# Sums of weight blocks made in the first token group, in 128 columns, in buffers of the raw operands

## The chip, the core and the metric

The kernel runs on one core of one Trainium2 chip. TensorE (PE in the profile; PEld is its weight load) multiplies matrices, VectorE (DVE) and ScalarE (ACT) work on rows of elements, GpSimd (POOL) and SyncE (SP) mostly start transfers here. All engines take their instructions in a fixed order and wait for each other by semaphores. The metric is the device time of one execution in microseconds (us).

## The reference

One step of a layer whose heads are of two kinds. 1024 prompt frames and 8 x 16 frames of running streams (with 1024 cached frames each) go through the same weights:

```python
h = rms_norm(x, norm_pre)
p = einsum('btd,de->bte', h, w_in)         # D = 2048, 8 x 1024 columns
q_sb, k_sb, v_sb, gate_sb, q_r, k_r, v_r, gate_r = split(p)   # 8 heads of 128 each
o_sb = stick_breaking(q_sb, k_sb, v_sb)    # exp(log sigmoid(z) + sum of later log sigmoid(-z)) @ v
o_r, s = retention(rope(q_r), rope(k_r), v_r)   # chunks of 64, decayed state 128 x 128 per head
y = concat(head_norm(o_sb) * silu(gate_sb), head_norm(o_r) * silu(gate_r))
x = x + rms_norm(einsum('bte,ed->btd', y, w_out), norm_post)
```

Keys, values and states are returned too.

## The kernel before

**Two groups of tokens.** Group 0 is prompt tiles 0 to 3 and the sample tile (640 columns, multiplied in pieces of 256 and 384), group 1 is prompt tiles 4 to 7 (512 columns). Each group goes through the 8 heads. A head has the projections of its eight weight columns, a stick-breaking attention and a retention; in group 0 also the decode against the cached frames. After group 1 the output projection follows.

**Projections.** A chunk of weights `wr` (128x512) is loaded by SP (L369, five buffers) and split into a high part `wh` (ACT, L166) and a low part `wl` (DVE, L167). `products` (L380) then does four steps with three products each: wh with the high and the low part of the rows (`mh`, `ml`) and wl with the high part. The rows' projection does the same with `wrn`, `whn`, `wln` (L422, L436), in 10 steps for the 5 tiles of group 0.

**Jobs.** Everything else is written as generators. `Job(gen, wait)` puts one on a list, and `tick()`, called after each product, advances one of them when its countdown has run out. A generator yields the number of ticks until its next step, so the pace constants (`D_...`) spread its instructions between the products. `drain(job)` runs what is left of a job at once. `pin` ties an instruction to the matmul where it was written, without a semaphore. A scheduler then settles the order of each engine when the kernel is compiled; it is fixed at run time.

**What stands near the change.** The attention of a head makes scores, a scan of them (DVE, L660), a product (L661) and a transpose `kp<-be` (L721) that feeds the second product `pa` (PE, L761); `so<-pa` (L764) copies the result out. Retention runs over four tiles: scores `rs` (PE, L891), `sc` (DVE, L893), the output `pa` (PE, L909 and L914 with the state S), its copy `ro<-pa` (L912, L918), the state's product `pS` (PE, L924) and S (L927, L929). It needs the small decay table `dT` (SP, L886) and keys that come back from DRAM in another layout (`ro<-s_rk`, SP, L624).

**The sums.** The output projection is done with seven products of blocks instead of eight (L1175 to L1179). It needs sums and differences of blocks of w_out and of the rows y. `sum_weights` (L266) gives one item: two loads from w_out into a tile `br` of four blocks, four DVE operations between the blocks, one store to the scratch `s_b`. `sum_rows` (L277) is the same for rows, to `s_s`. `sums` (L285) runs a list of items, with the next item's loads issued before the present one's operations:

```python
nxt = fetch(items[i + 1][0]) if i + 1 < len(items) else None
for o, a, b, how in ops:
    pin(nc.vector.tensor_tensor(r[:, o], r[:, a], r[:, b], ALU.add if how == "a" else ALU.subtract))
    yield pace[0]
yield pace[1]
pin(nc.scalar.dma_start(dst, r))
```

The job is started in the attention of group 1's head 0, with 32 weight items of 256 columns and the 8 items of group 0's rows between them. `first_left` (L1043), which makes operands of the output projection, drains it.

The tag `mr` in the pool `wp` is four buffers of 128x512 for raw operands: `load_moving` (L244) uses them for the normalised rows of group 1 (`mr<-s_h`, L250), and the output projection uses them again.

Of the kernel before, what the change touches and what calls it, by code (L numbers as in the profile page):

```python
# [11 lines left out]
F32 = mybir.dt.float32  # L12
# [6 lines left out]
P = 128  # L19
D = 2048  # L20
KT = D // P
H = 8
# [36 lines left out]
D_FIN = 2  # L59
D_MR = 6  # L60
D_OP = 2
D_SUM2 = (4, 6, 36)
D_SUM3 = (3, 3, 6)
MR = 4
# [27 lines left out]
def tile_hybrid_step(  # L92
# [141 lines left out]
    def drain(job):  # L234
        while job is not None and not job.done:
            tick()
# [27 lines left out]
            yield D_MR  # L264

    def sum_weights(k, c):  # L266
        cs = slice(c * 256, (c + 1) * 256)

        def load(r):
            for kk in range(2):  # L270
                rows = w_out[0, (kk * HT + k) * P : (kk * HT + k + 1) * P, :]
                pin(nc.sync.dma_start(r[:, 2 * kk : 2 * kk + 2], rows.rearrange("p (a n) -> p a n", a=2)[:, :, cs]))

        ops = ((0, 1, 0, "s"), (1, 3, 1, "s"), (3, 3, 0, "s"), (2, 3, 2, "s"))
        return load, ops, s_b[c // 2][k][:, :, (c % 2) * 256 : (c % 2 + 1) * 256]

    def sum_rows(gi, h):  # L277
        def load(r):
# [3 lines left out]
        ops = ((3, 1, 3, "a"), (1, 0, 1, "s"), (0, 3, 0, "s"), (2, 2, 0, "s"))  # L282
        return load, ops, s_s[gi][h]

    def sums(pool, items, pace, bufs):  # L285

        def fetch(load):
            r = pool.tile([P, 4, 256], F32, name="br", tag="br", bufs=bufs)
            load(r)
            return r  # L290

        r = fetch(items[0][0])
        yield pace[2]
        for i, (_, ops, dst) in enumerate(items):
# [6 lines that stand above are left out]
            r = nxt  # L301
            yield pace[2]
# [147 lines left out]
    with ExitStack() as s1:  # L450
# [590 lines left out]
            return [[half[i][:, h // 2, h % 2 * 256 : h % 2 * 256 + 256] for h in range(HT)] for half in mov]  # L1041

        def first_left():  # L1043
            drain(summed[0])
            mine["s", 0] = [[half[h // WQ][:, h % WQ, NB_TOK:] for h in range(HT)] for half in mov]
            yield from left_sample(0, *mine["s", 0], wp, "mr", MR)
            mine[0, 5] = kept(0)
            yield from left(0, 5, *mine[0, 5], wp, "mr", MR)

        ret_job = sb_job = sub = loads = after = None  # L1050
        for gi, g in enumerate(GROUPS):
            tiles, n, nt = g["tiles"], g["n"], len(g["tiles"])
            if gi == 1:
                mov = after
            if gi:
                load_rope(gi)
            off = 0 if gi == 0 else 4
            phase[0] = gi
            for h in range(H):
                rows_in = {}  # L1060

                def ret_queries():
                    nonlocal ret_job, loads
                    if h == 0:
                        ret_values(g, mov, h, loads)
                        loads = None
                    acc = project(g, mov, col(4, h))
                    drain(ret_job)
                    rows_in["rq"] = rope(acc, "rq", *ropes)

                def ret_keys():
                    nonlocal ret_job
                    rk = rope(project(g, mov, col(5, h)), "rk", *ropes)
                    rows_in["rest"] = {}
                    ret_job = Job(
                        ret_branch(gi, g, h, rows_in["rq"], rk, pair["r"][:, :, h % 2, :], rows_in["rest"]),
                        D_NAT[phase[0]],
                    )

                def ret_start():  # L1080
                    nonlocal ret_job
                    rows_in["rest"] = first[-1]
                    ret_job = Job(ret_branch(gi, g, h, *first), D_NAT[phase[0]])

                def ret_gate():
                    rows_in["rest"]["rg"] = gate(project(g, mov, col(7, h)), "rg")

                def attention():
                    nonlocal sb_job, sub, ip
                    acc = project(g, mov, col(0, h))  # L1090
                    held = project(g, mov, col(1, h)) if h == H - 1 else None
                    drain(sb_job)
                    if gi == 1 and h == 0:
                        drain(sub)
                        late.close()
                        banks.append(s1.enter_context(tc.tile_pool(name="psx", bufs=1, space=PSUM)))
                        ip = s1.enter_context(tc.tile_pool(name="ip2", bufs=1))
                        items = [sum_weights(k, c) for k in range(HT) for c in range(4)]
                        items[8:8] = [sum_rows(0, h) for h in range(H)]
                        summed.append(Job(sums(ip, items, D_SUM2, 2), 8))  # L1100
                        Job(residuals(), 150)
                    q2 = [kq.tile([P, NB_TOK], F32R, name=f"q{c}", tag=f"q{c}") for c in "hl"]
                    evac_split(acc, *q2)
                    qs = None
                    if SAMPLE in tiles:
                        qs = kq.tile([P, P], F32, name="qs", tag="qs")
                        nc.scalar.activation(qs, acc[1][0][:, 2 * P : 3 * P], AF.Copy)
                    out = Out(4, "so")
                    rest = rows_in["sb"] = {}
                    if SAMPLE in tiles:  # L1110
                        drain(sub)
                        sub = Job(decode(h, qs, rest), D_DEC)
                    acc = held or project(g, mov, col(1, h))
                    kT = kq.tile([P, NMAX], F32, name="kT", tag="kT")
                    for a, (o, m) in acc:
                        nc.scalar.activation(kT[:, o : o + m], a[:, :m], AF.Copy)
                    pool, n = (ip, PT * P) if gi else (kq, NB_TOK)
                    k2 = [pool.tile([P, n], F32R, name=f"k{c}", tag=f"k{c}") for c in "hl"]
                    evac_split(acc, *k2, off * P)
                    if gi == 1:  # L1120
                        kp = wp.tile([P, NB_TOK], F32, name="kpast", tag="mr", bufs=MR)
                        nc.sync.dma_start(kp, s_k[h])
                        split(k2[0][:, :NB_TOK], k2[1][:, :NB_TOK], kp)
                    rest["kT"] = kT
                    sb_job = Job(sb_branch(gi, g, h, out, q2, k2, kT, rest), D_NAT[phase[0]])
                    if h % 2 == 0:
                        pair["s"] = ep.tile([P, 8, 2, P], F32, name="vn", tag="vn")
                        project_rows(g, mov, col(2, h), pair["s"], off)
                    vn = pair["s"][:, :, h % 2, :]
                    if gi == 1:  # L1130
                        nc.sync.dma_start(vn[:, :4, :], s_v[h])
                    rest["vn"] = vn

                def gates():
                    nonlocal after, loads
                    if h < H - 1:
                        rows_in["sb"]["sg"] = gate(project(g, mov, col(3, h)), "sg")
                        return

                    after = [[], []]  # L1140
                    loads = first_left() if gi else load_moving(after, 0, NB_TOK, from_h)
                    if gi == 0:
                        next(loads)
                    accs = project_pair(g, mov, (col(7, h), col(3, h)), loads)
                    rows_in["rest"]["rg"], rows_in["sb"]["sg"] = gate(accs[0], "rg"), gate(accs[1], "sg")


                if (gi, h) == (0, 0):
                    order = ret_start, attention, gates
                elif gi == 0 or h < H - 3:  # L1150
                    order = ret_queries, ret_keys, ret_gate, attention, gates
                elif h == H - 3:
                    order = ret_queries, ret_keys, attention, ret_gate, gates
                elif h == H - 2:
                    order = ret_queries, attention, ret_keys, ret_gate, gates
                else:
                    order = attention, ret_queries, ret_keys, ret_gate, gates
                for panel in order:
                    if panel is not ret_gate or h < H - 1:
                        panel()  # L1160
                if h % 2 == 1 and h < H - 1:
                    ret_values(g, mov, h + 1)
# [377 lines left out]
```

## Time and profile before

| | |
|---|---|
| three runs | 2297.01, 2302.54, 2304.21 us; median 2302.54 |
| profiled execution | 2303.65 us, span 2301.9 us, mean granted clock 0.996 |
| busy: PE, DVE, ACT, POOL | 98%, 54%, 40%, 16% of the span |
| DMA | 462.61 MB, mean 201 GB/s |
| DVE sums (`br`, 128x256) | 192 instructions of 0.419 us (median), from 1182.7 to 2056.6 us |
| loads of w_out for them, stores to `s_b` | 64 on SP from 1173.9 us, 32 on ACT to 1871.3 us |

All times in views are microseconds from the span's start, durations in "ns" are named so. A row of a timeline has start, duration, engine, line, operation and the tiles (out<-in); a bracket at its end is how long the engine was idle before it, and what ended that. "x2" is two instructions together. A row of waits has the waiting engine and line, what released it, the total, the number of times and the longest.

### The profile page before, as it was taken

What the parts mean: (1) busy time and instruction counts of PE and PEld (TensorE: products, weight loads), DVE (VectorE), ACT (ScalarE), POOL (GpSimd) and SP (SyncE); (2) the same over time, 40 slices, a digit from 0 to 9 for tenths busy, and PEclk for the clock granted to TensorE, in tenths of its full rate; (3) what the DMA queues carried; (4) which work ended last, traced back from release to release, by engine and by line L of the source; (5) the groups of instructions that cost most, each with busy time, mean ns of one, the idle gap of its engine ahead of it and who ended that gap; (6) DMA issues with size and microseconds to landing.
All of it is one profiled execution on the core that took longest, in us unless ns stands there. A gap on an engine that the chain in (4) does not pass through costs nothing.

```text
span 2301.9 us, 39303 instructions
## 1 busy us (share of the span) xinstructions
PE 2261.7 (98%) x14496; PEld 2045.1 (89%) x14496; DVE 1231.9 (54%) x2541; ACT 919.7 (40%) x1951; POOL 356.8 (16%) x601
## 2 busy tenths in 40 slices
PE   7999999999999999999999999999999999999998
PEld 7999999999999999999888889898889987888886
DVE  7335445344444435355556565656565566556567
ACT  6333333333333333334433343343443444535363
POOL 3002020111203012021202111120212212000020
PEclk9999999999999999999999999999999999999999
DMA  7547547566566757568769777778787767766586
GB/s 251 167 154 220 183 148 234 172 185 198 152 195 183 211 160 203 181 175 262 226 201 231 216 214 234 221 221 222 226 228 217 213 168 183 241 219 185 148 207 186
DMA packets 446497, 462.61 MB, mean 201 GB/s; under 512 B 181984, under 2 KB 309984, under 8 KB 444640
## 3 DMA queue, kind: packets, MB, share of 16 engines
q1 hardware_dynamic: 315952, 295.69, 44.7%
q0 software_dynamic: 28720, 78.41, 12.1%
q10 hardware_dynamic: 101632, 86.00, 11.9%
q8 instruction: 113, 1.85, 0.3%
q14 instruction: 80, 0.66, 0.1%
HBM read 355.12 MB, written 114.29 MB: 204 GB/s over the span
## 4 chain that ended last, share of the span: by engine, by line
PE 87%; DMA 6%; DVE 4%; issue 1%; ACT 1%; SPq 1%; POOL 0%; DVEq 0%; ACTq 0%; POOLq 0%
PE acc L380 45%; PE accn L436 17%; PE a L1178 5%; PE a L1179 5%; PE a L1175 5%; PE z L731 2%; PE pa L761 2%; PE zc L800 1%; DMA s_o<-so 1%; PE pd L864 1%; DMA ro<-s_rk 1%; PE pa L909 1%; DMA dT<-c_dt 1%; PE pS L924 1%; DMA s_rk<-rk 1%
## 5 line engine op out<-in xcount | busy, mean ns | idle before, releaser
L380 PE MATMUL acc<-mh,wh 128*128 128x256 f32 (+2 forms) x2304 | 663.6, 340 | 0.0
L380 PE MATMUL acc<-ml,wh 128*128 128x256 f32 (+2 forms) x2304 | 659.8, 339 | 0.0
L380 PE MATMUL acc<-mh,wl 128*128 128x256 f32 (+2 forms) x2304 | 657.0, 338 | 0.0
L167 DVE TENSOR_TENSOR wl<-wr,wh 128x512 fp32r<-128x512 f32 x504 | 346.4, 690 | 497.5 <-ACT wh L166 477.9
L166 ACT ACTIVATE wh<-wr 128x512 fp32r<-128x512 f32 x504 | 317.3, 631 | 654.2 <-PE acc L380 341.8
L380 PEld LDWEIGHTS acc<-ml,wh 128*128 128x128 f32 x2304 | 422.1, 188 | 31.2 <-issue 3.3
L380 PEld LDWEIGHTS acc<-mh,wl 128*128 128x128 f32 x2304 | 424.4, 188 | 27.7
L380 PEld LDWEIGHTS acc<-mh,wh 128*128 128x128 f32 x2304 | 420.4, 188 | 31.6 <-issue 3.3
L436 PE MATMUL accn<-whn,mh 128*128 128x256 f32 x1152 | 329.8, 286 | 0.0
L436 PE MATMUL accn<-wln,mh 128*128 128x256 f32 x1152 | 326.0, 283 | 0.0
L436 PE MATMUL accn<-whn,ml 128*128 128x256 f32 x1152 | 325.6, 283 | 0.0
L436 PEld LDWEIGHTS accn<-whn,mh 128*128 128x128 f32 x1152 | 220.7, 192 | 3.0 <-issue 0.8
L436 PEld LDWEIGHTS accn<-wln,mh 128*128 128x128 f32 x1152 | 220.8, 192 | 0.8
L436 PEld LDWEIGHTS accn<-whn,ml 128*128 128x128 f32 x1152 | 220.5, 192 | 0.0
L167 DVE TENSOR_TENSOR wln<-wrn,whn 128x512 fp32r<-128x512 f32 x128 | 87.8, 688 | 152.4 <-ACT whn L166 151.1
L166 ACT ACTIVATE whn<-wrn 128x512 fp32r<-128x512 f32 x128 | 80.7, 633 | 192.9 <-PE accn L436 86.9
L624 POOL DMA_DIRECT2D be<-s_be x128 | 94.1, 742 | 148.2 <-DMA s_be<-be 125.3
L660 DVE TENSOR_TENSOR_SCAN kp<-kp 128x1152 f32<-128x1152 f32 (+4 forms) x40 | 82.8, 2069 | 51.5 <-POOL kp L649 35.0
L649 POOL TENSOR_SCALAR_AFFINE_SELECT kb<-kb 128x128 f32<-128x128 f32 x64 | 30.5, 484 | 451.2 <-ACT kb L643 448.9
L787 POOL DMA_DIRECT2D kcT<-cache_k x64 | 34.7, 545 | 422.7 <-PE pd L864 268.8
L1178 PE MATMUL a<-wl,mh 128*128 128x512 f32 x240 | 93.5, 390 | 0.0
L1179 PE MATMUL a<-wh,ml 128*128 128x512 f32 x240 | 93.6, 390 | 0.0
(257 smaller groups left out, 3001.9 us busy)
## 6 DMA issues: line engine op xcount, KB each, us to landing
wr<-w_cols SPq DMA_DIRECT2D x384, 256.0 KB, 4.3
wrn<-w_rows SPq DMA_DIRECT2D x128, 256.0 KB, 3.4
kcT<-cache_k POOLq DMA_DIRECT2D x64, 512.0 KB, 8.0
vc<-cache_v SPq DMA_DIRECT2D x64, 512.0 KB, 5.5
wr<-s_b SPq DMA_DIRECT2D x80, 256.0 KB, 4.4
br<-w_out SPq DMA_DIRECT2D x64, 256.0 KB, 5.2
s_b<-br ACTq DMA_DIRECT2D x32, 512.0 KB, 4.9
wr<-w_out SPq DMA_DIRECT2D x48, 256.0 KB, 3.9
```

The costliest lines, as they stand in the source:

```text
L166: nc.scalar.activation(hi, src, AF.Copy),
L167: nc.vector.tensor_tensor(lo, src, hi.bitcast(F32), ALU.subtract),
L380: last = nc.tensor.matmul(a[:, :m], lhs[:, j, :], rhs[w][:, j, o : o + m], start=(w == 0 and j == 0 and n == 0), stop=(w == KT // WQ - 1 a ...
L436: anchor[0] = nc.tensor.matmul(a, lhs[q][:, jj, ts], rhs[:, j, :], start=(w == 0 and j == 0 and n == 0 and t % 2 == 0), stop=(w == KT // 2 ...
L624: q.dma_start(raw[32 * i : 32 * i + 32, :].rearrange("p (k a) -> p k a", a=32), s[:, :, 32 * i : 32 * i + 32].rearrange("k (j b) a -> b (k ...
L660: nc.vector.tensor_tensor_scan(rev, rev, rev, 1.0, ALU.mult, ALU.bypass)
L731: nc.tensor.matmul(z[:, :c], q2[a][:, i * P : (i + 1) * P], k2[b][:, s : s + c], start=(m == 0), stop=(m == 2),)
L761: nc.tensor.matmul(po[:, :P], at[:, j, :], vn[:, j, :], start=(j == 0), stop=(j == t))
L787: ready.append((kc, nc.gpsimd.dma_start(kc, cache_k[h, m // 4, m % 4])))
L1175: ins = nc.tensor.matmul(a, hi[k][:, ts], wh, start=first, stop=False)
L1178: nc.tensor.matmul(a, hi[k][:, ts], wl, start=False, stop=False)
L1179: anchor[0] = nc.tensor.matmul(a, lo[k][:, ts], wh, start=False, stop=last)
```

## The change

The weight sums become 64 items of 128 columns instead of 32 of 256. Their tile is 128 x 4 x 128, the size of an `mr` buffer, and they take the four `mr` buffers in turn (tag "mr" in pool `wp`). They are started in the attention of group 0's head 1, with a pace of their own. In group 1's head 0 this job is drained, and there a second job is started for the 8 items of rows alone, as before in 128x256 with two buffers in the pool `ip2`. `first_left` drains that second job.

```diff
+D_SUM0 = (4, 4, 14)
 D_SUM2 = (4, 6, 36)
...
     def sum_weights(k, c):
-        cs = slice(c * 256, (c + 1) * 256)
+        cs = slice(c * P, (c + 1) * P)
...
-        return load, ops, s_b[c // 2][k][:, :, (c % 2) * 256 : (c % 2 + 1) * 256]
+        return load, ops, s_b[c // 4][k][:, :, (c % 4) * P : (c % 4 + 1) * P]
...
-    def sums(pool, items, pace, bufs):
+    def sums(pool, items, pace, bufs, tag="br", n=256):
...
-            r = pool.tile([P, 4, 256], F32, name="br", tag="br", bufs=bufs)
+            r = pool.tile([P, 4, n], F32, name="br", tag=tag, bufs=bufs)
...
         def first_left():
-            drain(summed[0])
+            drain(summed[1])
...
-                        items = [sum_weights(k, c) for k in range(HT) for c in range(4)]
-                        items[8:8] = [sum_rows(0, h) for h in range(H)]
-                        summed.append(Job(sums(ip, items, D_SUM2, 2), 8))
+                        drain(summed[0])
+                        summed.append(Job(sums(ip, [sum_rows(0, h) for h in range(H)], D_SUM2, 2), 8))
                         Job(residuals(), 150)
+                    if (gi, h) == (0, 1):
+                        items = [sum_weights(k, c) for k in range(HT) for c in range(8)]
+                        summed.append(Job(sums(wp, items, D_SUM0, MR, "mr", P), 8))
```

Lines of the changed kernel stand one higher than those of before in the code that the rows below name (L381 is L380).

**Group 0, head 2, TensorE.** Retention of this head, before; `acc` rows are products of weight chunks:

```order
L380 MATMUL acc_4505<-ml_174,wh 128x256
L380 MATMUL acc_4506<-ml_174,wh 128x384
L380 MATMUL acc_4505<-mh_173,wl 128x256
L380 MATMUL acc_4506<-mh_173,wl 128x384
L891 MATMUL rs<-rq,rk 128x128
L909 MATMUL pa<-rv,sc 128x128
L914 MATMUL pa<-S,rq 128x128
L380 MATMUL acc_4505<-mh_173,wh 128x256
```

After, at the same retention's first steps:

```order
L910 MATMUL pa<-rv,sc 128x128
L925 MATMUL pS<-rv,rkn 128x128
L892 MATMUL rs<-rq,rk 128x128
L910 MATMUL pa<-rv,sc 128x128
L915 MATMUL pa<-S,rq 128x128
L381 MATMUL acc_4382<-mh_179,wh 128x256
L381 MATMUL acc_4383<-mh_179,wh 128x384
L381 MATMUL acc_4382<-ml_180,wh 128x256
L381 MATMUL acc_4383<-ml_180,wh 128x384
L925 MATMUL pS<-rv,rkn 128x128
L381 MATMUL acc_4382<-mh_179,wl 128x256
```

Before, a step of retention (three or fewer short matmuls) stands between products of chunks that are under way; after, five short matmuls of two steps stand directly ahead of a chunk's first products, and pS of the second step inside it. Such places are found in heads 2 to 7 of group 0; those of group 1 are as before.

**The same place on VectorE**, before (`sg` is work of the finishing of another head):

```order
L893 TENSOR_TENSOR sc<-rs,dT 128x128 x2
L695 SCALAR_TENSOR_TENSOR sg<-kT,gains,sg 128x512
L912 COPY ro<-pa 128x128
L927 COPY S<-pS 128x128
L167 TENSOR_TENSOR wl<-wr,wh 128x512 x2
```

After:

```order
L894 TENSOR_TENSOR sc<-rs,dT 128x128 x2
L913 COPY ro<-pa 128x128
L928 COPY S<-pS 128x128
L894 TENSOR_TENSOR sc<-rs,dT 128x128
L168 TENSOR_TENSOR wl<-wr,wh 128x512 x2
L919 SCALAR_TENSOR_TENSOR ro<-pa,dec,ro 128x128
L168 TENSOR_TENSOR wl<-wr,wh 128x512
```

The score products and copies of two steps now stand together ahead of the `wl` conversions, and one more score product is among them.

**The loads ahead of that place, on SP's queue**, before (`ro`, `so` and `dT` belong to retention and to the finishing of heads; `vc` is the cached values):

```order
L827 DMA vc<-cache_v 128x1024 x2
L369 DMA wr<-w_cols 128x512 x2
L827 DMA vc<-cache_v 128x1024 x2
L369 DMA wr<-w_cols 128x512 x2
L624 DMA ro<-s_rk_2_4153 32x20x32 x4
L624 DMA so<-s_o_1_4_0_4233 32x16x32 x4
L886 DMA dT<-c_dt 128x256
L369 DMA wr<-w_cols 128x512 x2
L422 DMA wrn<-w_rows 128x512 x5
```

After:

```order
L273 DMA br<-w_out 128x2x128 x2
L828 DMA vc<-cache_v 128x1024 x2
L370 DMA wr<-w_cols 128x512
L273 DMA br<-w_out 128x2x128 x2
L370 DMA wr<-w_cols 128x512
L625 DMA ro<-s_rk_2_4218 32x20x32 x4
L625 DMA so<-s_o_1_4_0_4314 32x16x32 x4
L273 DMA br<-w_out 128x2x128 x2
L887 DMA dT<-c_dt 128x256
L370 DMA wr<-w_cols 128x512 x5
L423 DMA wrn<-w_rows 128x512 x4
```

The loads of w_out stand between the others, and ahead of `ro` there are two single `wr` loads where two pairs stood; behind `dT` there are five where two stood.

**Group 1, head 2, VectorE**, ahead of the transpose `kp<-be` 128x896, before:

```order
L474 TENSOR_TENSOR rq<-rq,sw 128x512
L297 TENSOR_TENSOR br<-br 128x256
L764 COPY so<-pa 128x128
L660 SCALAR_TENSOR_TENSOR kp<-kp 128x1024
L297 TENSOR_TENSOR br<-br 128x256
L661 TENSOR_TENSOR be<-be,kp 128x1024
L297 TENSOR_TENSOR br<-br 128x256
L721 STREAM_TRANSPOSE kp<-be 128x896
```

After:

```order
L475 TENSOR_TENSOR rq<-rq,sw 128x512
L765 COPY so<-pa 128x128
L168 TENSOR_TENSOR wl<-wr,wh 128x512
L661 SCALAR_TENSOR_TENSOR kp<-kp 128x1024
L639 MEMSET kp 128x1
L662 TENSOR_TENSOR be<-be,kp 128x1024
L722 STREAM_TRANSPOSE kp<-be 128x896
```

The three sums are gone, and a `wl` conversion stands ahead of the scan.

## The prediction

> **What bounds the kernel now.** I read the page's busy times first, then the busy table of two stretches, then TensorE's waits in them. The columns of the table are: the stretch, its length, busy time (and instructions) of PE, PEld, DVE, ACT and POOL, the granted clock, the busy share of the DMA engines, GB/s.
>
> ```profile
> PE 2261.7 (98%) x14496; PEld 2045.1 (89%) x14496; DVE 1231.9 (54%) x2541; ACT 919.7 (40%) x1951; POOL 356.8 (16%) x601
> 310.00:1060.00 750.00, 749.32 (x5727) 713.92 (x5726) 338.76 (x740) 263.03 (x569) 126.22 (x232) 1.00 0.63 187
> 1174.00:1870.00 696.00, 687.72 (x3947) 604.79 (x3946) 419.64 (x792) 270.66 (x562) 124.80 (x196) 1.00 0.79 220
> PE pa L761 <- DVE kp L721: 6.2, 5, 2.3
> PE pa L909 <- DVE so L764: 1.6, 2, 1.3
> PE pa L914 <- DVE S L929: 0.4, 1, 0.4
> ```
>
> TensorE is the bound: 98% busy, at full clock in both stretches. The first stretch is heads 1 to 7 of the first group. TensorE is idle there for 750.00 - 749.32 = 0.7 us. The second stretch is the second group while it makes the weight sums, and TensorE is idle for 696.00 - 687.72 = 8.3 us. The three last rows name nearly all of that: 6.2 + 1.6 + 0.4 = 8.2 us, always behind DVE, which is busy for 420 of 696 us there and for only 339 of 750 us in the first stretch. The change takes no matmul away. So it can gain at most about these 8.2 us, and it can lose wherever it makes TensorE wait in a stretch that has no waits yet.
>
> **What leaves the second group.** The work that moves:
>
> ```profile
> L297 DVE TENSOR_TENSOR br<-br x192: 379/419/514, 1182.7 to 2056.6; 128x256 f32<-128x256 f32 x192
> L272 SPq DMA_DIRECT2D br<-w_out x64: 540/602/1649, 1173.9 to 1843.1; - x64
> L300 ACTq DMA_DIRECT2D s_b<-br x32: 520/582/1346, 1190.2 to 1871.3; - x32
> ```
>
> Of the 192 DVE instructions 4 x 32 = 128 are weight sums (the other 64 sum rows, and stay): 128 x 0.419 = 53.6 us of DVE. That is almost all of the second stretch's surplus. What it is worth is read where TensorE waits, at the transpose that feeds the second product of the attention:
>
> ```profile
> 1265.79 1.25 DVE L721 STREAM_TRANSPOSE kp<-be 128x1024 f32<-128x1024 f32 x1 [3.58 <-DMA be<-s_be]
> ...
> 1345.51 0.42 DVE L297 TENSOR_TENSOR br<-br 128x256 f32<-128x256 f32 x1
> 1345.85 0.28 DVE L764 COPY so<-pa 128x128 f32<-128x128 f32 x1
> 1346.05 2.28 DVE L660 TENSOR_TENSOR_SCAN kp<-kp 128x1024 f32<-128x1024 f32 x1
> 1348.25 0.40 DVE L297 TENSOR_TENSOR br<-br 128x256 f32<-128x256 f32 x1
> 1348.56 1.22 DVE L661 TENSOR_TENSOR be<-be,kp 128x1024 f32<-128x1024 f32 x1
> 1349.70 0.42 DVE L297 TENSOR_TENSOR br<-br 128x256 f32<-128x256 f32 x1
> 1350.04 1.10 DVE L721 STREAM_TRANSPOSE kp<-be 128x896 f32<-128x896 f32 x1
> ...
> 1454.39 0.69 DVE L167 TENSOR_TENSOR wl<-wr,wh 128x512 fp32r<-128x512 f32 x1 [1.24 <-DMA br<-w_out]
> 1351.19 1.05 PE L761 MATMUL pa<-vn,kp 128*128 128x128 f32 x7 [0.74 <-DVE kp L721]
> ...
> 1459.68 1.50 PE L761 MATMUL pa<-vn,kp 128*128 128x128 f32 x11 [1.06 <-DVE kp L721]
> ```
>
> Three sums stand in the chain from copy to transpose of head 2 (0.42 + 0.40 + 0.42 = 1.24 us). In the new order a 0.69 us wl conversion moves up into that gap, so the chain shortens by about 0.55 and not by 1.24. At head 3 DVE even stands still for 1.24 us in a sum that waits for its load. That and the sums around it are more than the 1.06 us for which TensorE waits. Of the 6.2 us the longest wait, 2.3, has no sum in its chain: its transpose stood idle for a load, be<-s_be (first row). Of the other 3.9 I take 3.2. The copy so<-pa stands right behind a sum as well, so I take 1.2 of its 1.6. **Gain: 4.4 us**, with bounds 0 (each chain keeps another late link) and 8.2 (all waits go, the 2.3 by a quicker load once 33.5 MB less share the DMA engines).
>
> **What comes into the first group.** 64 items of 128 columns: 256 DVE instructions, 128 loads on SP, 64 stores on ACT, the same bytes. One item takes 4 x 4 + 4 + 14 = 34 ticks. The list starts at head 1's attention, near 300 us. The rows for its cost:
>
> ```profile
> L893 DVE TENSOR_TENSOR sc<-rs,dT 128x128 f32<-128x128 f32 x28 | 7.3, 278 | 12.0 <-PE rs L891 9.9 <-DMA dT<-c_dt 2.1
> L167 DVE TENSOR_TENSOR wl<-wr,wh 128x512 fp32r<-128x512 f32 x140 | 96.4, 689 | 181.0 <-ACT wh L166 180.1 <-PE rs L891 0.9
> L167 DVE TENSOR_TENSOR wln<-wrn,whn 128x512 fp32r<-128x512 f32 x42 | 29.1, 692 | 75.0 <-ACT whn L166 74.8
> L166 ACT ACTIVATE wh<-wr 128x512 fp32r<-128x512 f32 x140 | 88.3, 631 | 233.9 <-PE acc L380 166.2 <-PE accn L436 35.3 <-DMA wr<-w_cols 11.6
> wr<-w_cols SPq DMA_DIRECT2D x384, 256.0 KB, 4.3
> out<-vn ACTq DMA_DIRECT2D x16, 256.0 KB, 3.2
> out<-kT ACTq DMA_DIRECT2D x16, 256.0 KB, 4.1
> ```
>
> A wl chunk is 12 ticks and a wln chunk 10, so the 140 and the 42 of these rows are 1680 + 420 = 2100 ticks in 750 us, 0.357 each. An item is then 12.1 us, and the list 775: over near 1075, ahead of 1173.9, where it only began before.
>
> - DVE: a 128x128 operation takes 0.278, so 256 x 0.278 = 71 us, 18 more than leave. With 339 + 71 = 410 of 750 us DVE is as full as it is in the second group now. Cost taken: nothing by itself, since the wl conversions wait 180 us for ACT and not for DVE.
> - ACT: 64 issues at 0.52 to 0.58 (the store's shortest and median above) are 33 to 37 us beside 263 of 750. Nothing, for the wh conversions wait for TensorE to free buffers (166.2).
> - SP: 128 issues at 0.54 to 0.60, or 69 to 77 us, in a queue that also carries every weight load. They can delay those loads; the bunches below price that.
> - DMA: 33.5 MB in 775 us is +43 GB/s on 187, and the busy share goes from 0.63 to about 0.63 x 230/187 = 0.78, the second group's level now. Rows of 512 bytes in the sums are no surcharge: the vn store writes such rows and takes 3.2 us, the kT store of equal size with 2 KB rows 4.1.
>
> Order shows one thing that the counts don't. From head 2 on, retention stands in a bunch right ahead of a weight chunk, with that chunk's wl behind the retention's own work on DVE. There are six such places (heads 2 to 7). Before, this work was spread between products:
>
> ```profile
> 375.41 7.35 SPq L624 DMA_DIRECT2D ro<-s_rk  x4
> 382.86 2.04 SPq L624 DMA_DIRECT2D so<-s_o  x4
> 384.94 0.49 SPq L886 DMA_DIRECT2D dT<-c_dt  x1
> 395.18 0.39 PE L909 MATMUL pa<-rv,sc 128*128 128x128 f32 x2
> 395.40 0.39 PE L924 MATMUL pS<-rv,rkn 128*128 128x128 f32 x2
> 395.60 0.29 DVE L912 COPY ro<-pa 128x128 f32<-128x128 f32 x1 [1.55 <-PE pa L909]
> 395.82 0.29 DVE L927 COPY S<-pS 128x128 f32<-128x128 f32 x1
> 1167.78 0.49 PE L909 MATMUL pa<-rv,sc 128*128 128x128 f32 x2 [0.31 <-DVE ro L918]
> ```
>
> The price of one bunch. After pS, DVE has the two copies (0.29 each), a score product (0.28) and the wl conversion (0.69): 1.55 us. TensorE meanwhile has three short matmuls (0.22 from one start to the next, 395.18 to 395.40) and two ticks of 0.357: 1.37 us. So it waits 0.2, and the one bunch of this kind in the trace waits 0.31 (last row). 0.3 is the lower end. If the chunk's wh is not ready either, 0.63 is added: 0.9. If a second and a third conversion stand behind it as well, 2 x 0.69 more: 2.3. I take 0.9: wr loads now stand in the queue behind ro, so and dT, which hold SP for 375.41 to 385.4, about 10 us, so wh loses its head start. **Loss: 6 x 0.9 = 5.4 us**, with bounds 1.8 and 13.8.
>
> At the boundary of the groups the first four mr<-s_h loads now wait for the sums' buffers; the last w_out loads stand ahead of them and the wait for the list costs no tick. I take nothing (0 to 1.5).
>
> **Sum.** -4.4 + 5.4 = +1.0. The profiled run took 2303.65 us (span 2301.9), so it would become 2304.7. That run lies 1.1 us above the median of 2302.54. I name 2304, between the sums from either. About 0.3%, or 6.9 us, is what a measurement of this kernel can tell from no change.
>
> **The rivals.**
> - A, faster: the first group hides everything, bunches too, and the second loses all its waits. 2303.65 - 8.2 = 2295.4. For it: 0.7 us of idle time in 750. Against: the bunches are in the order, and nothing stands behind the wl there.
> - B, slower: weights become late at the bunches. The next chunk's wr stands behind the held queue, and its head start must cover landing 4.3 plus wh 0.63 = 4.9 us. Five buffers of 12 ticks are 5 x 4.3 = 21 us of head start at most. The new order has three such loads fewer ahead of the held entries: 21 - 13 = 8 us is left. It decides when the entries hold SP for 3 to 4 us longer than their 10 now. The price of one wait of that length is in the clock as well:
>
> ```profile
> 1932.01 0.49 PE L909 MATMUL pa<-rv,sc 128*128 128x128 f32 x2 [2.05 <-DVE so L764]
> 1932.00:1937.00 5.00, 5.00 (x20) 4.23 (x21) 1.67 (x5) 2.59 (x10) 2.73 (x4) 0.66 0.79 172
> ```
>
>   After a wait of 2.05 us the clock (the column after POOL's) was 0.66 for the next 5 us: 0.34 x 5 = 1.7 us more. Six waits of 2.1 cost 6 x 3.8 = 22.8, less the gain 4.4: +18, or 2322.
>   The Trainium skill (TensorE: Matmul & The Clock Gate, Part 1) says that the clock is lowered only after a whole idle window of some 3.4 us. By that the six waits would cost 6 x 2.1 = 12.6 and the case +8. The clock fell after 2.05 us here, so the measurement decides and the 1.7 stay in.
> - C, slower: the first group takes over the second's way of waiting, since DVE (410 of 750) and DMA (0.78) come to the same level. 8.2 us in 696 become 9.1 in 775; with the bunches 5.4 and the gain 4.4 that is +10, or 2314. Against: its attention chains are shorter (four tiles of rows with at most 512 keys), so fewer transposes come late.
> - That the change does nothing isn't open: order moves all 64 items ahead of the boundary.
>
> **How the numbers follow.** The forecast, within 0.3%, gets 0.42: its own range is 2297 to 2309. A gets 0.18, B 0.22, C 0.18. B is likelier than C because its rows stand in the order. Low: 2295, which takes A's point in. High: 2322, B's point; half of B and a little of A lie outside, under 2 in 10. Faster 0.18, same 0.42, slower 0.22 + 0.18 = 0.40.
>
> **What would show it.** Right: in the second group the waits of pa for kp fall to the 2.3 of head 1 and something under 1; in the first group six waits of 0.3 to 2.3 us before L381 or pa, for wl or S; a DMA share near 0.78. Wrong: waits of L381 for wh behind wr<-w_cols of over 2 us with a granted clock of 0.66 after them (B); waits for kp and so spread over heads 1 to 7 (C); no waits in the first group at all (A).

## The result

The changed kernel took 2338.82 us in the median of four runs (2333.81 to 2344.24), the kernel before 2301.01 us. The ratio is 1.0157, with a 95% interval from 1.0137 to 1.0178: slower by 38 us by the medians and 36 by the ratio, outside the range that was given and beyond rival B.

The span and the busy line of the changed kernel's page (its profiled execution took 2344.24 us):

```profile
span 2342.5 us, 39517 instructions
PE 2276.4 (97%) x14496; PEld 2056.6 (88%) x14496; DVE 1241.6 (53%) x2669; ACT 918.6 (39%) x1951; POOL 359.8 (15%) x601
```

Two stretches of its busy table, columns as in the prediction. The first lies in the first group, the second in the second group, without weight sums:

```profile
310.00:1085.00 775.00, 751.40 (x5634) 713.20 (x5634) 382.69 (x960) 256.75 (x557) 124.39 (x228) 0.98 0.74 215
1200.00:1900.00 700.00, 692.28 (x4015) 606.74 (x4014) 377.20 (x680) 273.23 (x574) 125.39 (x195) 1.00 0.63 174
```

The span grew by 2342.5 - 2301.9 = 40.6 us. TensorE's idle time went from 2301.9 - 2261.7 = 40.2 us to 2342.5 - 2276.4 = 66.1 us, which is 25.9 of it. The other 14.7 us are busy time of the same 14496 matmuls, at a lower clock (0.98 in the first stretch). The loss lies in the first group: 775.00 - 751.40 = 23.6 us idle there. The second group is idle for 7.7 us, where it was 8.3.

TensorE's waits in the whole changed kernel, without those of the start; columns as in the prediction:

```profile
PE pa L910 <- DVE sc L894: 23.1, 6, 5.7
...
PE pa L762 <- DVE kp L722: 7.2, 5, 3.3
PE acc L381 <- ACT wh L167: 3.8, 3, 2.4
```

Six waits of retention's output matmul for its scores `sc`, one in each of heads 2 to 7, make 23.1 us. They are at the places that order had shown, but for another reason than the one named. Here is head 2 in the changed kernel's timeline:

```profile
375.19 6.97 SPq L625 DMA_DIRECT2D ro<-s_rk  x4
382.33 3.35 SPq L625 DMA_DIRECT2D so<-s_o  x4
385.73 3.97 SPq L273 DMA_DIRECT2D br<-w_out  x2
389.74 0.60 SPq L887 DMA_DIRECT2D dT<-c_dt  x1
...
395.43 0.49 DVE L894 TENSOR_TENSOR sc<-rs,dT 128x128 f32<-128x128 f32 x2 [3.80 <-DMA dT<-c_dt]
395.78 0.80 PE L910 MATMUL pa<-rv,sc 128*128 128x128 f32 x2 [4.73 <-DVE sc L894]
396.04 0.63 ACT L167 ACTIVATE wh<-wr 128x512 fp32r<-128x512 f32 x1 [6.27 <-DMA wr<-w_cols]
```

VectorE and ScalarE have nothing to do: VectorE waits 3.80 us for the table dT, ScalarE 6.27 us for a weight chunk. dT is issued at 389.74, where the kernel before issued it at 384.94, and it lands 5.6 us later where it took 3.5. The transfers are late, not an engine's work.

A part of each wait comes from TensorE's own order. Counted in the two traces, retention's first `pa` stands 13 matmuls of `acc` and `accn` earlier in the changed kernel, in each of heads 2 to 7. From 375 to 395 the kernel before has 119 of these matmuls in 20 us, so 13 are about 2.2 us (an estimate). With `pa` at its old place and dT as late as here, about 11 of the 23.1 us would be left. No run changes this place alone.

A long wait can be paid twice. The busy table of the changed kernel, 5 us from the end of a wait on, after the waits of 4.73, 0.95, 2.37 and 4.13 us:

```profile
395.80:400.80 5.00, 5.00 (x22) 5.00 (x23) 4.04 (x11) 3.27 (x9) 0.00 (x0) 0.53 0.73 229
...
810.90:815.90 5.00, 2.52 (x16) 2.01 (x16) 1.45 (x6) 1.29 (x5) 0.00 (x0) 1.00 0.60 196
816.00:821.00 5.00, 5.00 (x24) 5.00 (x25) 3.58 (x9) 2.10 (x5) 0.00 (x0) 0.66 0.84 289
951.90:956.90 5.00, 4.96 (x21) 4.96 (x22) 4.04 (x11) 3.27 (x9) 0.00 (x0) 0.51 0.71 229
```

The clock is whole after 0.95 us, 0.66 after 2.37, and about a half after more than 4. There are six such places (five at waits for sc, one at the wait for wh). Over the 5 us behind each they had a clock of 0.53, 0.67, 0.50, 0.66, 0.51 and 0.50, which loses 13.2 us, most of the 14.7.

### The profile page after: what moved, and what is told of

Its sections match the earlier page's. It is cut to its first block, busy times and chain, and to the rows that moved or that the text cites. A ratio compares the mean times of both kernels' runs of the same rounds, so it can differ in the third digit from the quotient of the medians.

```text
span 2342.5 us, 39517 instructions
## 1 busy us (share of the span) xinstructions
PE 2276.4 (97%) x14496; PEld 2056.6 (88%) x14496; DVE 1241.6 (53%) x2669; ACT 918.6 (39%) x1951; POOL 359.8 (15%) x601
## 4 chain that ended last, share of the span: by engine, by line
PE 83%; DMA 8%; DVE 4%; issue 2%; ACT 2%; SPq 1%; ACTq 0%; POOL 0%; DVEq 0%; POOLq 0%
PE acc L381 42%; PE accn L437 17%; PE a L1181 5%; PE a L1182 5%; PE a L1178 5%; PE pa L762 2%; DMA wr<-w_cols 2%; PE z L732 2%; DMA dT<-c_dt 2%; PE zc L801 1%; DMA s_o<-so 1%; PE pa L910 1%; DMA s_b<-br 1%; DVE wl L168 1%; PE pS L925 1%
## 5 line engine op out<-in xcount | busy, mean ns | idle before, releaser
L381 PE MATMUL acc<-mh,wh 128*128 128x256 f32 (+2 forms) x2304 | 663.8, 341 | 4.9 <-ACT wh L167 3.8
L381 PE MATMUL acc<-ml,wh 128*128 128x256 f32 (+2 forms) x2304 | 661.0, 340 | 0.0
L381 PE MATMUL acc<-mh,wl 128*128 128x256 f32 (+2 forms) x2304 | 660.3, 340 | 0.0
L381 PEld LDWEIGHTS acc<-mh,wh 128*128 128x128 f32 x2304 | 423.3, 189 | 37.5 <-ACT wh L167 4.5
L381 PEld LDWEIGHTS acc<-ml,wh 128*128 128x128 f32 x2304 | 424.5, 189 | 30.3 <-issue 2.1
L381 PEld LDWEIGHTS acc<-mh,wl 128*128 128x128 f32 x2304 | 424.4, 189 | 29.1 <-issue 1.2
L298 DVE TENSOR_TENSOR br<-br 128x128 f32<-128x128 f32 (+1 forms) x320 | 99.9, 313 | 7.0 <-DMA br<-s_y 4.0
```

What stands on the lines that cost most here:

```text
L381: last = nc.tensor.matmul(a[:, :m], lhs[:, j, :], rhs[w][:, j, o : o + m], start=(w == 0 and j == 0 and n == 0), stop=(w == KT // WQ - 1 a ...
```

## The experiments

All ratios are to the kernel before, with 95% intervals. The first theory was that SP's queue is the cause: 128 loads of w_out stand in it ahead of dT and the weights.

**Loads on another queue.**

```diff
-                pin(nc.sync.dma_start(r[:, 2 * kk : 2 * kk + 2], rows...
+                pin(nc.gpsimd.dma_start(r[:, 2 * kk : 2 * kk + 2], rows...
```

> The changed kernel with the 128 loads of w_out for the sums issued by GpSimd and not by SyncE; operations, stores and bytes are the same. Theory Q (the six waits of TensorE for sc come from SP's queue: the loads of w_out stand ahead of dT, ro and wr there and hold them up): no wait of pa for sc over 1 us is left in the first group, and the time is 2297 to 2306. Rival D (the 43 GB/s more on the DMA engines make dT and wr land late, whoever issues them): the waits stay, 2325 to 2345. Rival V (256 operations more on VectorE in the first group): the waits stay, 2325 to 2345.

2336.3 us, ratio 1.015 (1.0132 to 1.0168). The theory of SP's queue fell. The waits in the first group:

```profile
PE pa L910 <- DVE sc L894: 26.2, 6, 5.5
```

In this kernel's order the bunches of the first group are gone as well: no place there has more than three matmuls of retention in a row, and the first `pa` stands within 2 matmuls of its old place. Two weight loads stand right ahead of ro, as before the change. SP's rows in head 2:

```profile
371.25 0.86 SPq L370 DMA_DIRECT2D wr<-w_cols  x2
372.16 12.35 SPq L625 DMA_DIRECT2D ro<-s_rk  x4
384.62 4.43 SPq L625 DMA_DIRECT2D so<-s_o  x4
389.09 0.56 SPq L887 DMA_DIRECT2D dT<-c_dt  x1
```

The landing times of dT in heads 2 to 7 (least, median, greatest, in us):

```profile
DMA to landing us min/median/max: 7.7/8.3/11.7
```

In head 2 the four issues of ro took 12.35 us, where they took 7.35 in the kernel before. The median landing of dT was 8.3 us, where it was 5.3. So late transfers make waits of this size without the bunches and without loads of w_out in SP's queue. What the bunches cost in the changed kernel is not measured by that.

**Loads alone.**

```diff
-                pin(nc.vector.tensor_tensor(r[:, o], ...
+                n == P or pin(nc.vector.tensor_tensor(r[:, o], ...
...
-            pin(nc.scalar.dma_start(dst, r))
+            n == P or pin(nc.scalar.dma_start(dst, r))
```

> The changed kernel with the loads of w_out alone: the 256 operations and the 64 stores of the weight sums are left out, and the output projection reads single blocks of w_out where it read sums (as many bytes). Q: the loads alone make the waits for sc, 2320 to 2342; if a good part of them is a load waiting for a store's semaphore, nearer to 2320. V: no waits, 2297 to 2304. D: half the bytes are gone, so half of the loss, 2315 to 2322.

2327.18 us, ratio 1.0104 (1.0082 to 1.0126). Half of the bytes, without any operation, make 24 of the 36 us; the waits for sc are 17.4 us. A cause on VectorE alone is out, and the loss is not simply in proportion to the bytes. The first `pa` of retention stands 13 matmuls earlier in this kernel too, so a part of the 24 us can be that.

**Stores on another queue.**

```diff
-            pin(nc.scalar.dma_start(dst, r))
+            pin((nc.gpsimd if n == P else nc.scalar).dma_start(dst, r))
```

> The changed kernel with the 64 stores of weight sums issued by GpSimd and not by ScalarE. The loads of w_out on SP wait for stores s_b<-br (17.8 us, 9 times in the first group). Theory L (loads on SP and stores on ACT take turns on shared semaphores, and a load waits for the store before it to land): these waits are gone, the waits for sc fall from 23 us to under 12, and the time is 2315 to 2325. Rival Q alone (the order of SP's queue): the waits stay, 2333 to 2344.

2336.66 us, ratio 1.0148 (1.0128 to 1.0169). The waits of SP's loads of w_out for stores (17.8 us) are gone from its trace, and the waits for sc are still 24.9 us. Shared semaphores are not the cause.

**No weight sums at all**, in either group (the job and its drain taken out).

> The kernel without any weight sums, in either group: loads, operations and stores are left out, and the output projection reads single blocks of w_out where it read sums (as many bytes); row sums as in the changed kernel. This is the whole gain that taking them from the second group can bring. My step in the prediction (DVE's sums make the waits for kp and so): 4.4 us under before, about 2296.6. Theory O (the waits for kp are set by the place of pa in TensorE's order, some 1.06 us behind the transpose whatever else VectorE does): 0 to 2 us under before, 2299 to 2301, with waits for kp of 1.06 us as in the changed kernel.

2299.59 us, ratio 0.9983 (0.9972 to 0.9994): 3.9 us under before by the ratio (1.4 to 6.4). This is all that there was to gain. TensorE's waits in this kernel's second group, from 1172 to 1868 us:

```profile
PE pa L762 <- DVE kp L722: 5.9, 5, 2.1
PE pa L915 <- DVE S L930: 0.2, 1, 0.2
```

The waits for kp are 5.9 us, and were 6.2 with the sums. What went in this stretch is the wait for so (1.6).

**Where in a head.** The mean share of the DMA engines hides how they are loaded over a head. The kernel before, head 2 of the first group (the last two columns are the share of the DMA engines and GB/s):

```profile
335.00:340.00 5.00, 5.00 (x37) 3.24 (x37) 2.45 (x3) 2.02 (x4) 2.11 (x3) 1.00 0.25 90
345.00:365.00 20.00, 20.00 (x140) 20.00 (x140) 9.60 (x21) 6.45 (x15) 1.60 (x3) 1.00 0.92 257
375.00:395.00 20.00, 20.00 (x157) 18.88 (x156) 9.11 (x25) 6.99 (x12) 2.17 (x5) 1.00 0.99 300
```

From 375 to 395, where ro, so, dT and the next weights are loaded, the engines are full already, 0.99, without any sums. TensorE does not notice. In head 2 dT lands some 6.7 us ahead of its `pa` (388.4 and 395.18). In head 6 it lands just in time: VectorE waits for it, and TensorE not yet:

```profile
921.71 0.49 DVE L893 TENSOR_TENSOR sc<-rs,dT 128x128 f32<-128x128 f32 x2 [1.07 <-DMA dT<-c_dt]
```

This gave theory B: what falls into this burst lengthens it. Two kernels set the items into the two parts of a head:

```diff
+            while not part[0] <= (clock[0] - begin) % 368 < part[1]:
+                yield 2
             nxt = fetch(items[i + 1][0]) if i + 1 < len(items) else None
```

> The changed kernel with the same 64 items, but an item begins only in the first 195 of the 368 ticks of each head (from some 265 us on in the first head), faster there (pace 2, 1, 8). In those ticks the DMA engines of the kernel before are 0.2 to 0.5 busy; in the rest of a head they are at 0.85 to 1.1 for some 45 us. Theory B (the loss comes from transfers of sums that lengthen this burst, in which so, dT and wr are loaded): no wait for sc over 1 us, and the gain of the second group stays, 2296 to 2303. Rival T (the sums cost the same wherever they stand in the first group, by bytes, by SP's instructions or by VectorE): 2325 to 2342.

2305.37 us, ratio 1.0012 (1.0002 to 1.0022). All 64 items are still in the first group, and 33 of the 36 us are gone. The time is above theory B's range all the same: two waits for sc of 1.6 us are left, and the kernel without sums is 6.7 us faster by the ratios. Retention is back at its old place here (within 2 matmuls), so the bunches went together with the traffic in the burst.

> The opposite: the same 64 items begin only in ticks 210 to 358 of each head (pace 2, 2, 7), where the DMA engines are full without them. B: longer waits for dT and wr than in the changed kernel, 2345 to 2390. T: as the changed kernel, 2330 to 2344.

2417.27 us, ratio 1.0493 (1.0477 to 1.0509): slower by 5%, with the same items, operations and bytes, and outside theory B's range as well. Nine items begin in each of heads 2 to 7, and the rest at the boundary of the groups. The waits in the first group, of the quiet kernel and then of the other:

```profile
PE pa L913 <- DVE sc L897: 3.2, 2, 1.6
```

```profile
PE acc L384 <- ACT wh L167: 85.7, 6, 15.0
PE pa L913 <- DVE sc L897: 5.8, 5, 2.1
```

In the second kernel it is the weights that come late, 14.3 us a time. ScalarE and SP in its head 2:

```profile
396.79 0.63 ACT L167 ACTIVATE wh<-wr 128x512 fp32r<-128x512 f32 x1 [10.81 <-DMA wr<-w_cols]
...
375.37 7.24 SPq L628 DMA_DIRECT2D ro<-s_rk  x4
382.72 7.29 SPq L628 DMA_DIRECT2D so<-s_o  x4
390.11 3.13 SPq L273 DMA_DIRECT2D br<-w_out  x2
393.29 7.48 SPq L373 DMA_DIRECT2D wr<-w_cols  x7
```

SP in the kernel before, at the same place:

```profile
374.16 1.20 SPq L369 DMA_DIRECT2D wr<-w_cols  x2
```

The weights are late here because SP issues them late. The kernel before issues two right ahead of ro. This one issues none from 347 to 393, and then seven behind ro, so and loads of the sums. In heads 3 to 7, too, the first weight load is issued 13 to 18 us behind the first of ro. The one that ScalarE waits for landed 3.5 us after its issue, sooner than the two of before (6.9 and 8.7). dT, too, landed sooner than in the changed kernel (4.3 to 5.7 us from its issue). Slow transfers can have an indirect part: the four issues of so took 7.29 us, where they took 2.04 before.

So theory B is borne out for the quiet kernel, up to the 3 us that are left. The second kernel shows another price: that of weight loads which stand behind the burst in SP's order. It does not price bytes on full DMA engines. Nine items of 512 KB would take 16 us at the 300 GB/s of the full stretch, by an estimate, but that is not what was waited for.

**dT out of the way.** dT of the next head is loaded at the end of this head's retention.

> The changed kernel with the table dT of the next head loaded at the end of this head's retention, some 60 us earlier; everything else as changed. Rival S (dT alone is late, since it stands last in the queue): the waits for sc go and nothing takes their place, 2298 to 2308. B (the whole queue lands late in the burst, dT is only the first to be missed): TensorE then waits for wh behind wr or for pS behind rkn, 2318 to 2338.

2325.18 us, ratio 1.0099 (1.0085 to 1.0113). It takes back 13 us of the 36; no wait for dT is left. The waits of the first group move on to the weights, as B had it:

```profile
PE acc L381 <- ACT wh L167: 8.2, 6, 2.4
PE pa L918 <- DVE ro L927: 1.5, 3, 0.6
```

dT was only the first transfer to be missed.

**Operations alone**, on one tile over and over, without loads and stores.

> The changed kernel with the 256 operations of the weight sums alone in the first group: after the first tile's two loads the items work on that tile over and over, nothing more is loaded and nothing stored, and the output projection reads single blocks of w_out. Rival V (71 us more on VectorE in the first group cost something of their own): 2305 to 2320. Theory B (only transfers matter): as without any sums, 2295 to 2302, no wait for sc over 1 us.

2305.45 us, ratio 1.0007 (0.9998 to 1.0016). That is the lower end of rival V's range and above theory B's, 5.5 us (by the ratios) above the kernel without sums. Its trace has three waits for sc, 5.8 us in all, and two of them behind a dT that took 7 and 10 us to land. Whether the operations make them, or a changed order of transfers does, this run can't tell. It bounds VectorE's part at some 5 of the 40 us between the changed kernel and the one without sums.

**Half of the dose.**

```diff
-                        summed.append(Job(sums(wp, items, D_SUM0, MR, "mr", P), 8))
+                        summed.append(Job(sums(wp, items[:32], (8, 8, 28), MR, "mr", P), 8))
```

> The changed kernel with half of the dose: 32 of the 64 items in the first group at half the pace (8, 8, 28: one item in 24 us), the other 32 in the second group at the pace 4, 4, 14. B with a price (bytes that fall into the burst at the full rate of 394 GB/s: one item is 512 KB read and written together, about 1.7 of them fall into a head's burst in the changed kernel, so 0.9 of them here, 1.1 us each): waits of 1 to 3 us a head in place of 4 to 6, 2308 to 2322. Rival (a threshold: below some load the burst ends in time): 2300 to 2304.

2310.67 us, ratio 1.0031 (1.0015 to 1.0048). Half of the items cost 7 us (3 to 11) and not 18. In its profiled execution, one of its quicker ones (2306.27), the first group has one wait for sc (2.3 us) and two for wh (1.7). Some slack in the burst, into which the first transfers go, would explain it. But retention's first `pa` stands near its old place in this kernel (2 matmuls earlier to 8 later), so the run does not tell slack from order.

**A try at a better version**: 32 items in the quiet part at a gentle pace, 32 in the second group.

> Half of the items in the first group, only in the first 185 ticks of a head and at a gentle pace (4, 4, 16), the other 32 items spread over the second group (4, 6, 36). A try at a version under both kernels: with no traffic of sums in the burst and less on VectorE in the second group, 2298 to 2301. If the waits of the quiet kernel at 1172 and 1274 us come from the fast pace, they are gone. If the second group's gain can't be had in halves, 2301 to 2304.

2304.97 us, ratio 1.0003 (0.9993 to 1.0012). The profiled execution has no wait of TensorE in the first group and took 2298.29, but over twelve runs it is not under the kernel before, and it misses both expected ranges.

**The waits for kp.** More ticks between the transpose and its product, in the kernel before:

```diff
-D_TR = (12, 7)
+D_TR = (12, 13)
```

> The kernel before with 13 ticks, not 7, between the transpose of the last two row tiles and their product in the second group (D_TR; sums as before). Theory O (the waits of pa for kp are set by its place in TensorE's order, not by what else VectorE does): the four waits of about 1 us go, 3 to 4 us under before, 2297 to 2300. My step in the prediction (the sums on VectorE make them): they become shorter at most by the ticks given and come back at the next place, 2300 to 2304.

2303.56 us, ratio 1.0005 (0.9997 to 1.0014): no change. The waits for kp are 5.2 us, where they were 6.2, and the same product now waits for a copy of retention as well. Its timeline still has the same wait of 1.06 us:

```profile
1455.68 1.83 PE L761 MATMUL pa<-vn,kp 128*128 128x128 f32 x14 [1.06 <-DVE kp L721]
```

The new waits of that product:

```profile
PE pa L761 <- DVE ro L918: 5.2, 2, 4.4
```

A wait of 1.06 us stands at this product in the kernel before, in the changed one and in the one without sums. So the sums don't make it, though the time lies in the range of my step; but giving ticks doesn't remove it either, and theory O is not shown. What sets it is open.

## Why the prediction was wrong

- **The DMA term failed.** The prediction put the traffic at "0.63 to about 0.78" and let it cost nothing, as the second group's level. The mean came out at 0.74, close to that. But the mean was the wrong measure: the question was what the engines do from 375 to 395 in a head, and the answer, 0.99, stood in the trace of before. What came in place of nothing were the six waits for dT, 23.1 us, and 14.7 us of lower clock, some of both with the bunches' help. Two kernels show that the transfers matter: with the loads on GpSimd, without bunches and without loads of w_out on SP, TensorE still waits 26.2 us; with the items outside of the burst all but 3 of the 36 us are gone.
- **The bunches: right places, wrong price.** Six waits were forecast in heads 2 to 7, 0.9 us each for wl and wh; there were six, 3.9 us each, for dT. The price counted conversions. It left out that a bunch asks for dT earlier, by the 2.2 us of the estimate above. The kernel without bunches waits just as long, with dT still later, so the share of the bunches stays open.
- **Rival B had the chain but not the price.** dT, held up by other transfers, and the clock falling after the wait are both there. B took 2.1 us and 1.7 us of clock each; measured are 3.9 and about 14.7 / 6 = 2.5. Its condition was SP's entries held for 3 to 4 us longer. dT was issued 4.8 us later, and landed 2.1 us slower on top. The loads of w_out in SP's queue are not needed for that, since with them on GpSimd the issues of ro held SP even longer (12.35 us). B's own step, weights behind the held entries, is what the kernel with its items in the burst shows, at 14.3 us a time.
- **The clock.** The Trainium skill (TensorE: Matmul & The Clock Gate, Part 1) has a free-running window of some 3.4 us, and half speed after an idle one. By an estimate from these two figures, half speed for 3.4 of 5 us gives a clock of 0.66, and that is what the rows show after 2.37 us. That a whole window has to be idle is not what the rows show: the clock fell after 2.37 us here and after 2.05 before. Nor does such a wait always cost clock: after 2.33 us in the kernel with half of the items and after 2.82 in the one with loads alone it was 1.00 over the next 5 us. So B's 1.7 us is not a fixed price of a wait of 2 us.
- **The gain was about right in size, by the wrong waits.** 4.4 us were forecast for the second group, 3.9 is the whole gain without sums. But 3.2 of the 4.4 were to come from kp, and kp's waits fell by 0.3. In the changed kernel (1200 to 1900) they even rose, from 6.2 to 7.2, the longest from 2.3 to 3.3; the wait for so went. The row with three sums ahead of a late transpose showed what stood near the wait, not what made it. The row of 1.24 us at head 3 was misread: it is a wl conversion, not a sum, that stands behind the idle time.
- **VectorE and ScalarE at nothing, SP within the bunches' price**: borne out within 5 us for VectorE (operations alone). With ScalarE's stores on GpSimd the time changed by 2 us, with SP's loads there by 3 at most. But the order of the engines changed with the loads, so SP's own part is not separated.

## What to carry to other kernels

A mean DMA share doesn't show the room for more transfers. Cut the period of the loop (here a head) into stretches of 5 to 20 us. Where the share is near 1.0, ask which load has the least time to spare, and expect added transfers to make that one late first. Then read two places in the new order: where the weight loads stand in the issuing queue, and where the matmul stands that needs the late load. If work has to move, place it by that table: the same 64 items cost 3 us in the quiet part of a head, 36 spread evenly, and 114 in the burst, each with the order that its kernel got.

## What was not expected of the hardware

A stretch's median landing time doesn't show such a burst. The landing times (least, median, greatest, in us) in the first group from 310 to 1085, of weight chunks wr in the kernel before and in the changed one:

```profile
DMA to landing us min/median/max: 2.9/4.3/11.0
```

```profile
DMA to landing us min/median/max: 2.8/4.1/10.7
```

They are alike. Those of dT, before and changed, are not:

```profile
DMA to landing us min/median/max: 3.5/5.3/7.7
```

```profile
DMA to landing us min/median/max: 5.0/7.9/9.8
```

Weight loads that are issued in the burst are slow without any sums (6.9 and 8.7 us at 374.16 in the kernel before), and the median over all of them hides it. What the sums made later was dT, and the kernel stopped for that. Whether a landing is long because of bytes, of their many small pieces or of the order in which queues are served, no run here tells apart.
